# Moving the gated delta rule's elementwise work from GpSimd to VectorE: all of it in layer 0, three operations in layer 1

## The chip, the cores and the metric

The kernel runs on one core of a Trainium2 chip. A core has a matrix engine (TensorE, PE in the profile), a vector engine (VectorE, DVE), an engine for activations and copies (ScalarE, ACT), a general engine (GpSimd, POOL) and a queue that starts the loads of weights (SyncE, SP). Each engine works through its own instructions strictly in the order in which they were put down; semaphores make one engine wait for another. The metric is the time of one execution on the device in microseconds: the median of three executions of the kernel before is 1779.97 us (1774.64 to 1780.54).

## What is computed

Two layers of a diffusion backbone over 256 context tokens and 256 latent tokens, 1024 channels, all in float32. In each layer a modulated RMS norm is projected at once to the inputs of three mixers (latent attention, windowed attention, and a bidirectional gated delta rule); their outputs are gated, merged and projected, and a gated MLP with a depthwise convolution follows. The change is in the delta rule alone. It works on chunks of 64 tokens, 8 heads of 64 channels, forwards and backwards:

```python
gam = jnp.cumsum(g, axis=-1)
decay = jnp.exp(jnp.minimum(gam[..., :, None] - gam[..., None, :], 0.0))
a_mat = jnp.where(strict, jnp.einsum('nbhid,nbhjd->nbhij', kb, k) * decay, 0.0)   # kb = k * beta
t_mat = a_mat + jnp.eye(C)
wy = triangular_solve(t_mat, rhs, left_side=True, lower=True, unit_diagonal=True)
qk = jnp.where(incl, jnp.einsum('nbhid,nbhjd->nbhij', q, k) * decay, 0.0)
def step(S, xs):                                   # over the 4 chunks
    v_new = u_c - w_c @ S
    o = (q_c * exp(gam_c)) @ S + qk_c @ v_new
    S = S * exp(g_last) + (k_c * exp(g_last - gam_c)).T @ v_new
y = rmsnorm(o, o_norm) * silu(z)
```

## The kernel before, in words

**Projections.** Weights come by DMA into `raw` tiles (three buffers, mostly 128x1024). ScalarE rounds each to `wh` (L189), VectorE makes the remainder `wl = raw - wh` (L179, four buffers), and TensorE forms each product from three matmuls (L199 to L201: `wh` times the high part of the activations, `wh` times the low part, `wl` times the high part). L201 can't start on a tile before VectorE has made its `wl`. Accumulators are in PSUM, 3 buffers named `mm` and 5 named `g`.

**Delta rule.** Streams `s` are the context (0) and the latent tokens (1). `gdn_decay(s)` runs over two halves `tl` and two phases `ph`: `rg` (L803) spreads the log decays, a matmul (L808) sums them, L809 takes the difference `d` out of PSUM, L813 to L816 make the masked decays `Eq` for q·k, L819 to L821 those for k·k, L824 makes `bm` (mask times beta), `times_k` multiplies 64x64 products of keys into a tile (matmuls L839; the multiplication is on the line of a helper, L131), and L828 forms `N = d*bm`. `gdn_solve(s)` inverts the unit triangular matrices: VectorE transposes `N` in 32x32 blocks, runs a chain of 60 dependent multiply and add operations on `gtmp` and `W`, transposes back, TensorE joins the blocks (matmuls L877 and L905), and L915 scales the result `XT` by beta. `gdn_scan(s)` takes 4 steps: the state product (matmul L935, L938 and L940 on VectorE), `pvn` (matmul L951), `vp` (L955), the decay of the state (L958), its update (matmul L965, addition L970), and the output (matmuls L980, L985 and L986). `gdn_out` scales the output rows (L1009) ahead of the transposes L1014. A layer needs `qk` for the context only if it isn't the last.

**The order of the work.** These parts are generators that yield a number of microseconds; `chain` puts that much projection work (the "filler", with its loads and splits) between two parts, so TensorE has matmuls while VectorE computes the decays. Each engine's final order comes from a scheduler that goes by the tiles' dependencies and by priorities: `times_k` and the transposes and chain of `gdn_solve` are recorded through a helper with a raised priority, so that the profile puts them on the helper's line, L131. Where a group of the profile has line L131 with tiles `s<-s,g` of 128x512 it is `times_k`'s multiplication; with `gtmp` it is the solve's chain. The delta rule of layer 0 stands between about 86 and 405 us of the profile, that of layer 1 between about 1175 and 1405 us.

## Time and profile before

| what | value |
|---|---|
| median of three executions | 1779.97 us (1774.64 to 1780.54) |
| the profiled execution | 1780.76 us, its span 1779.0 us |
| TensorE | 1679.0 us busy, mean granted clock 0.968 |
| VectorE | 1133.4 us busy |
| ScalarE | 769.2 us busy |
| GpSimd | 300.4 us busy, 281 instructions |

TensorE is busy nearly throughout, so the places that count are those where it waits, or where it runs at a lower granted clock. An engine's mean load over the span says little about a stretch; the windows show each engine's busy time stretch by stretch, the waits show for whom TensorE stood still, and the rows in time show what VectorE did meanwhile.

### The profile page before, as it was taken

The numbers are of one execution on the slowest core, as the hardware profiler recorded it, in microseconds if no ns is written. First come the engines' busy times: TensorE is split into PE (matmuls) and PEld (weight loads), VectorE is DVE, ScalarE is ACT, GpSimd is POOL, SyncE is SP. The second block draws the span as 40 slices with busy tenths as digits, with TensorE's granted clock in tenths as the row PEclk, the third lists the DMA queues.
The fourth block names the chain that finished last, engine by engine and source line by source line (L and its number), as shares of the span: only waits on it lengthen the run. The fifth ranks groups of instructions, "written<-read, shape, count | busy, mean of one in ns | idle before, by whom it ended". The sixth has DMA issues, their size and how long they took to land. (4 is left out here: it accounts for less than half of the span.)

```text
span 1779.0 us, 31557 instructions
## 1 busy us (share of the span) xinstructions
PE 1679.0 (94%) x12723; PEld 1363.7 (77%) x12723; DVE 1133.4 (64%) x2159; ACT 769.2 (43%) x1371; POOL 300.4 (17%) x281
## 2 busy tenths in 40 slices
PE   7989988999999999999999999999898899999997
PEld 4768765776556888768888888778787667999997
DVE  3897595474865643545535553699796776677684
ACT  3644312233755333324313432464523475555463
POOL 1040411221200222001100112030502310213010
PEclk8999998998999999999999999999998999999999
DMA  9423326333043633663333343434352223745663
GB/s 346 115 72 107 96 73 190 72 75 111 25 143 122 210 119 120 253 231 96 98 95 103 95 141 120 125 92 141 90 120 58 60 77 98 236 144 182 185 185 124
DMA packets 216944, 228.75 MB, mean 129 GB/s; under 512 B 51228, under 2 KB 195422, under 8 KB 215646
## 3 DMA queue, kind: packets, MB, share of 16 engines
q1 hardware_dynamic: 211582, 220.11, 40.5%
q10 hardware_dynamic: 4928, 6.56, 1.0%
q8 instruction: 100, 1.64, 0.4%
q14 instruction: 46, 0.38, 0.1%
q0 software_dynamic: 288, 0.06, 0.0%
HBM read 213.85 MB, written 11.80 MB: 127 GB/s over the span
## 5 line engine op out<-in xcount | busy, mean ns | idle before, releaser
L179 DVE TENSOR_TENSOR wl<-raw,wh 128x1024 fp32r<-128x1024 f32 (+2 forms) x294 | 364.3, 1239 | 250.2 <-ACT wh L189 248.6
L189 ACT CAST wh<-raw 128x1024 fp32r<-128x1024 f32 (+2 forms) x294 | 298.4, 1017 | 422.3 <-PE mm L200 220.5
L199 PE MATMUL mm<-xnh,wh 128*128 128x512 f32 (+2 forms) x1072 | 380.3, 356 | 5.8 <-ACT wh L189 2.4
L201 PE MATMUL mm<-xnh,wl 128*128 128x512 f32 (+2 forms) x1072 | 375.9, 353 | 1.3 <-DVE wl L179 1.3
L200 PE MATMUL mm<-xnl,wh 128*128 128x512 f32 (+2 forms) x1072 | 376.0, 351 | 0.1
L199 PEld LDWEIGHTS mm<-xnh,wh 128*128 128x128 f32 (+1 forms) x1072 | 206.3, 193 | 39.4 <-issue 7.0
L201 PEld LDWEIGHTS mm<-xnh,wl 128*128 128x128 f32 (+1 forms) x1072 | 205.9, 192 | 31.5 <-issue 3.3
L200 PEld LDWEIGHTS mm<-xnl,wh 128*128 128x128 f32 (+1 forms) x1072 | 206.1, 192 | 27.8 <-issue 2.9
L199 PE MATMUL g<-xnh,wh 128*128 128x256 f32 (+1 forms) x496 | 167.3, 340 | 1.4 <-ACT xnh L405 1.4
L200 PE MATMUL g<-xnl,wh 128*128 128x256 f32 (+1 forms) x496 | 166.4, 337 | 0.2 <-DVE xnl L406 0.2
L201 PE MATMUL g<-xnh,wl 128*128 128x256 f32 (+1 forms) x496 | 166.1, 336 | 0.0
L201 PE MATMUL mm<-s,wl 128*128 128x256 f32 (+1 forms) x458 | 150.0, 328 | 0.6 <-DVE wl L179 0.6
L199 PE MATMUL mm<-s,wh 128*128 128x256 f32 (+1 forms) x458 | 150.1, 329 | 0.4 <-DVE s L534 0.3
L200 PE MATMUL mm<-s,wh 128*128 128x256 f32 (+1 forms) x458 | 149.6, 327 | 0.1
L1616 POOL TENSOR_TENSOR b<-b,b 128x512 f32<-128x512 f32 (+1 forms) x44 | 54.3, 1234 | 442.5 <-DVE b L1600 381.6
L199 PEld LDWEIGHTS g<-xnh,wh 128*128 128x128 f32 x496 | 94.6, 192 | 15.0 <-issue 3.3
L199 PE MATMUL g<-s,wh 128*128 128x512 f32 (+1 forms) x304 | 102.8, 338 | 0.0
L201 PEld LDWEIGHTS g<-xnh,wl 128*128 128x128 f32 x496 | 94.6, 191 | 10.5 <-issue 1.2
L200 PEld LDWEIGHTS g<-xnl,wh 128*128 128x128 f32 x496 | 94.7, 191 | 10.1 <-DVE xnl L406 0.8
L200 PE MATMUL g<-s,wh 128*128 128x512 f32 (+1 forms) x304 | 102.2, 336 | 0.0
L201 PE MATMUL g<-s,wl 128*128 128x512 f32 (+1 forms) x304 | 102.2, 336 | 0.0
L199 PEld LDWEIGHTS mm<-s,wh 128*128 128x128 f32 x458 | 87.2, 191 | 8.8 <-DVE s L534 1.1
(285 smaller groups left out, 2743.6 us busy)
## 6 DMA issues: line engine op xcount, KB each, us to landing
raw<-in_w_in_dram SPq DMA_DIRECT2D x92, 512.0 KB
raw<-in_ffn_up_dram SPq DMA_DIRECT2D x80, 512.0 KB
s<-in_w_mod_dram SPq DMA_DIRECT2D x64, 512.0 KB
raw<-in_w_mod_dram SPq DMA_DIRECT2D x32, 512.0 KB
raw<-in_ffn_down_dram SPq DMA_DIRECT2D x32, 512.0 KB
raw<-in_w_out_dram SPq DMA_DIRECT2D x16, 512.0 KB
raw<-in_ffn_down_dram SPq DMA_DIRECT2D x16, 384.0 KB
spill<-s SPq DMA_DIRECT2D x4, 1024.0 KB
```

The source lines that it names most:

```text
L179: self.nc.vector.tensor_tensor(out=out, in0=x, in1=h.bitcast(F32), op=ALU.subtract)
L189: nc.scalar.copy(H, raw)
L199: mm(ps, lhsT=wH, rhs=xH, start=start, stop=False)
L200: mm(ps, lhsT=wH, rhs=xL, start=False, stop=False)
L201: mm(ps, lhsT=wL, rhs=xH, start=False, stop=stop)
L1616: nc.gpsimd.tensor_tensor(out=y[:, cs], in0=y[:, cs], in1=av[t][:, cs], op=ALU.mult)
```

## The change

A method `side()` returns VectorE in layer 0 and GpSimd in layer 1 (`narrow` is set at the start of a layer and is true in the last). The operations L803, L816, L824, L958 and L985 go through it, so they change engine in layer 0 alone. L828, L915 and L1009 are written for VectorE in both layers. The memory clears of the solve (L892) stay on GpSimd, as do the operations of attention and of the norms. In numbers, 50 instructions change engine in layer 0 (8 each of L803, L816, L824 and L915, 6 of L958, 4 each of L828, L985 and L1009) and 14 in layer 1 (4 of L828, 8 of L915, 2 of L1009). From the new method on, a line of the changed kernel has a number larger by 4: L828 is L832 there.

```diff
--- before.py
+++ after.py
@@ -792,6 +792,10 @@
         self.gt = dict(g=g, be=be, si=si, so=so, sk=sk, gam=gam, eg=eg, ekl=ekl, egl=ev)
         yield 2.0
 
+    def side(self):
+
+        return self.nc.gpsimd if self.narrow else self.nc.vector
+
     def gdn_decay(self, s, has_q):
 
         nc, gt = self.nc, self.gt
@@ -800,7 +804,7 @@
         for tl in range(2):
             rg = self.b4([128, 2, 8, 64])
             for ph in range(2):
-                nc.gpsimd.tensor_tensor(out=rg[:, ph], in0=gt["g"][:, s, ph, tl, :].unsqueeze(2).to_broadcast([128, 8, 64]),
+                self.side().tensor_tensor(out=rg[:, ph], in0=gt["g"][:, s, ph, tl, :].unsqueeze(2).to_broadcast([128, 8, 64]),
                                         in1=self.con(f"triJ{ph}").unsqueeze(1).to_broadcast([128, 8, 64]), op=ALU.mult)
             d = self.b4([128, 2, 8, 64])
             for ph in range(2):
@@ -813,7 +817,7 @@
                 self.pri(nc.vector, "hpd").tensor_scalar(out=Eq, in0=d, scalar1=0.0, scalar2=None, op0=ALU.max)
                 self.pri(nc.scalar, "hpd").activation(out=Eq, in_=Eq, func=AF.Exp, scale=-1.0)
                 for ph in range(2):
-                    nc.gpsimd.tensor_tensor(out=qk[:, tl, ph], in0=Eq[:, ph],
+                    self.side().tensor_tensor(out=qk[:, tl, ph], in0=Eq[:, ph],
                                             in1=self.con(f"mincl{ph}").unsqueeze(1).to_broadcast([128, 8, 64]), op=ALU.mult)
             for ph in range(2):
                 self.pri(nc.vector, "hpd").tensor_scalar(out=d[:, ph], in0=d[:, ph], scalar1=self.con("sgn")[:, ph:ph + 1], scalar2=0.0,
@@ -821,11 +825,11 @@
             self.pri(nc.scalar, "hpd").activation(out=d, in_=d, func=AF.Exp)
             bm = self.b4([128, 2, 8, 64])
             for ph in range(2):
-                nc.gpsimd.tensor_tensor(out=bm[:, ph], in0=gt["be"][:, s, ph, tl, :].unsqueeze(2).to_broadcast([128, 8, 64]),
+                self.side().tensor_tensor(out=bm[:, ph], in0=gt["be"][:, s, ph, tl, :].unsqueeze(2).to_broadcast([128, 8, 64]),
                                         in1=self.con("nms").unsqueeze(1).to_broadcast([128, 8, 64]), op=ALU.mult)
             yield self.P["dec1"]
             self.times_k(s, tl, 0, d)
-            nc.gpsimd.tensor_tensor(out=N[:, tl], in0=d, in1=bm, op=ALU.mult)
+            nc.vector.tensor_tensor(out=N[:, tl], in0=d, in1=bm, op=ALU.mult)
             yield self.P["dec2"]
 
     def times_k(self, s, tl, which, t):
@@ -912,7 +916,7 @@
                 self.evac(q, Xv[qs, tl, ph, :, 1 - q % 2, :], pq[qs, tl])
         for ph, tl in STEPS:
             hs = slice(ph * 64, ph * 64 + 64)
-            nc.gpsimd.tensor_tensor(out=XT[hs, tl, ph], in0=XT[hs, tl, ph],
+            nc.vector.tensor_tensor(out=XT[hs, tl, ph], in0=XT[hs, tl, ph],
                                     in1=gt["be"][hs, s, ph, tl, :].unsqueeze(2).to_broadcast([64, 8, 64]), op=ALU.mult)
         yield self.P["sol4"]
 
@@ -955,7 +959,7 @@
                 self.pri(nc.vector, "hps").tensor_tensor(out=vp, in0=pvn, in1=bc("sk"), op=ALU.mult)
                 Sn = self.b2([128, 2, 4, 64])
                 if St is not None:
-                    nc.gpsimd.tensor_tensor(out=Sn, in0=St, in1=gt["egl"][:, s, ph, tl].unsqueeze(3).to_broadcast([128, 2, 4, 64]), op=ALU.mult)
+                    self.side().tensor_tensor(out=Sn, in0=St, in1=gt["egl"][:, s, ph, tl].unsqueeze(3).to_broadcast([128, 2, 4, 64]), op=ALU.mult)
                 for hf in range(2):
                     hs = slice(hf * 64, hf * 64 + 64)
                     psu = self.ps([128, 4, 64], "g")
@@ -982,7 +986,7 @@
                     t = self.b2([128, 8, 64])
                     state_product(1, t)
                     if n >= 2:
-                        nc.gpsimd.tensor_tensor(out=t, in0=t, in1=o3, op=ALU.add)
+                        self.side().tensor_tensor(out=t, in0=t, in1=o3, op=ALU.add)
                     self.pri(nc.vector, "hps").tensor_tensor(out=o3, in0=t, in1=pqk, op=ALU.add)
                 else:
                     self.pri(nc.vector, "hps").tensor_copy(o3, pqk)
@@ -1006,7 +1010,7 @@
         self.rstd(r, ss, 1.0 / 64, [128, 2, 8])
         nc.vector.tensor_tensor(out=r, in0=r, in1=qr, op=ALU.mult)
         for tl in range(2):
-            nc.gpsimd.tensor_tensor(out=hd(oacc[:, tl, :]), in0=hd(oacc[:, tl, :]), in1=r[:, tl, :].unsqueeze(2).to_broadcast([128, 8, 64]), op=ALU.mult)
+            nc.vector.tensor_tensor(out=hd(oacc[:, tl, :]), in0=hd(oacc[:, tl, :]), in1=r[:, tl, :].unsqueeze(2).to_broadcast([128, 8, 64]), op=ALU.mult)
         yield Lat(self.P["w_o"])
         for tl in range(2):
             pf = self.ps([128, 4, 128], "g")
@@ -1294,7 +1298,7 @@
         nc, i = self.nc, self.ins
         if l:
             self.P = dict(P, **P["l1"])
-        last = l == DEPTH - 1
+        last = self.narrow = l == DEPTH - 1
         lat, full = slice(S, T), slice(0, T)
         oc = lat if last else full
         n = self.qw = S if last else T
```

The scheduler's order changes with it. On VectorE, in the first decay of layer 0, before: the second pair of `times_k`'s multiplications, the transposes of `N` (`s_141`), and two splits of weights (`wl_1125`, `wl_1161`); `s_171` is the solve's `W`.

```order
L131 TENSOR_TENSOR s_159_875<-s_159_875,g_911 128x8x64
L131 TENSOR_TENSOR s_159_875<-s_159_875,g_921 128x8x64
L131 STREAM_TRANSPOSE s_171_966<-s_141_768 128x1024
L665 SCALAR_TENSOR_TENSOR b_170_958<-mm_847,vec_86,b_170_958 128x2x255
L131 STREAM_TRANSPOSE s_171_966<-s_141_768 32x1024
L667 SCALAR_TENSOR_TENSOR b_170_958<-mm_847,vec_86,b_170_958 128x2x255
L131 STREAM_TRANSPOSE s_171_966<-s_141_768 32x1024
L179 TENSOR_TENSOR wl_1125<-raw_1122,wh_1124 128x1024
L131 TENSOR_TENSOR gtmp_970<-s_171_966 128x30
L699 TENSOR_REDUCE sm_1019<-b_181_1020 128x8
L131 TENSOR_TENSOR s_171_966<-s_171_966,gtmp_970 128x30
L699 TENSOR_REDUCE sm_1019<-b_182_1023 128x8
```

And the same place in the changed kernel:

```order
L179 TENSOR_TENSOR wl_1125<-raw_1122,wh_1124 128x1024
L820 TENSOR_TENSOR s_142_769<-s_162_882,cst 128x512 x2
L131 TENSOR_TENSOR s_159_875<-s_159_875,g_911 128x8x64
L131 TENSOR_TENSOR s_159_875<-s_159_875,g_921 128x8x64
L699 TENSOR_REDUCE sm_1019<-b_181_1020 128x8
L832 TENSOR_TENSOR s_141_768<-s_159_875,s_163_890 128x1024
L699 TENSOR_REDUCE sm_1019<-b_182_1023 128x8
L131 STREAM_TRANSPOSE s_171_966<-s_141_768 128x1024
L346 TENSOR_SCALAR sm_1028<-sm_1019 128x16
L131 STREAM_TRANSPOSE s_171_966<-s_141_768 32x1024 x2
L347 TENSOR_SCALAR sm_1029<-sm_1028 128x16
L179 TENSOR_TENSOR wl_1161<-raw_1158,wh_1160 128x1024
```

The first of the two splits, formerly behind the transposes, is now ahead of them, the second is still behind them, and `N` (L832) and the masked decays (L820) are in VectorE's own row; L699 has moved ahead of the transposes.

On VectorE, in the second decay of layer 0 and at the start of the scan, before: `s_297` is `d`, `s_142` and `s_282` are the `qk` of the two streams, `s_281` is `N`, and L955 is the scan's `vp`.

```order
L131 TENSOR_TENSOR s_297_1927<-s_297_1927,g_1973 128x8x64
L131 STREAM_TRANSPOSE s_325_2121<-s_281_1854 128x1024
L131 TENSOR_TENSOR s_142_769<-s_142_769,g_2008 128x8x64
L131 TENSOR_TENSOR s_142_769<-s_142_769,g_2018 128x8x64
L131 TENSOR_TENSOR s_142_769<-s_142_769,g_2028 128x8x64
L131 TENSOR_TENSOR s_142_769<-s_142_769,g_2038 128x8x64
L131 TENSOR_TENSOR s_282_1855<-s_282_1855,g_2048 128x8x64
L131 TENSOR_TENSOR s_282_1855<-s_282_1855,g_2058 128x8x64
L131 TENSOR_TENSOR s_282_1855<-s_282_1855,g_2068 128x8x64
L131 TENSOR_TENSOR s_282_1855<-s_282_1855,g_2078 128x8x64
L131 STREAM_TRANSPOSE s_325_2121<-s_281_1854 32x1024 x2
L955 TENSOR_TENSOR b_327_2150<-g_2089,gtb_754 128x512
```

The changed kernel:

```order
L131 TENSOR_TENSOR s_282_1855<-s_282_1855,g_2068 128x8x64
L131 TENSOR_TENSOR s_282_1855<-s_282_1855,g_2078 128x8x64
L131 TENSOR_TENSOR s_297_1927<-s_297_1927,g_1963 128x8x64
L131 TENSOR_TENSOR s_297_1927<-s_297_1927,g_1973 128x8x64
L959 TENSOR_TENSOR b_327_2150<-g_2089,gtb_754 128x512
L832 TENSOR_TENSOR s_281_1854<-s_297_1927,s_301_1942 128x1024
L179 TENSOR_TENSOR wl_2236<-raw_2233,wh_2235 128x1024
L131 STREAM_TRANSPOSE s_325_2121<-s_281_1854 128x1024
L972 COPY b_328_2152<-g_2153 128x256
L131 STREAM_TRANSPOSE s_325_2121<-s_281_1854 32x1024 x2
L972 COPY b_328_2152<-g_2163 128x256
```

`times_k`'s eight multiplications for `qk` now come first, then the pair for `N`, then the scan's `vp` (L959), and the transposes stand behind it and behind a split.

On VectorE, in the second decay of layer 1: `s_1898` is `d`, `s_1879` is `N`, `s_1880` is `qk`.

```order
L131 TENSOR_TENSOR s_1898_11316<-s_1898_11316,g_11372 128x8x64
L131 TENSOR_TENSOR s_1898_11316<-s_1898_11316,g_11382 128x8x64
L179 TENSOR_TENSOR wl_11521<-raw_11518,wh_11520 128x1024
L131 STREAM_TRANSPOSE s_1923_11505<-s_1879_11225 128x1024
L131 TENSOR_TENSOR s_1880_11226<-s_1880_11226,g_11448 128x8x64
L131 TENSOR_TENSOR s_1880_11226<-s_1880_11226,g_11458 128x8x64
L131 TENSOR_TENSOR s_1880_11226<-s_1880_11226,g_11468 128x8x64
L131 TENSOR_TENSOR s_1880_11226<-s_1880_11226,g_11478 128x8x64
L131 STREAM_TRANSPOSE s_1923_11505<-s_1879_11225 32x1024 x2
L955 TENSOR_TENSOR b_1930_11536<-g_11488,gtb_10178 128x512
```

The changed kernel:

```order
L131 TENSOR_TENSOR s_1898_11316<-s_1898_11316,g_11372 128x8x64
L131 TENSOR_TENSOR s_1898_11316<-s_1898_11316,g_11382 128x8x64
L179 TENSOR_TENSOR wl_11521<-raw_11518,wh_11520 128x1024
L832 TENSOR_TENSOR s_1879_11225<-s_1898_11316,s_1902_11331 128x1024
L131 TENSOR_TENSOR s_1880_11226<-s_1880_11226,g_11448 128x8x64
L131 TENSOR_TENSOR s_1880_11226<-s_1880_11226,g_11458 128x8x64
L131 TENSOR_TENSOR s_1880_11226<-s_1880_11226,g_11468 128x8x64
L131 TENSOR_TENSOR s_1880_11226<-s_1880_11226,g_11478 128x8x64
L131 STREAM_TRANSPOSE s_1923_11505<-s_1879_11225 128x1024
L959 TENSOR_TENSOR b_1930_11536<-g_11488,gtb_10178 128x512
L131 STREAM_TRANSPOSE s_1923_11505<-s_1879_11225 32x1024 x2
```

The multiplications for `qk` now come before the first transpose, and `vp` (L959) before the other two.

## Rows read from the trace of the kernel before

**Rows 1.** The page, part 1: busy time of each engine, share, instructions.

```profile
PE 1679.0 (94%) x12723; PEld 1363.7 (77%) x12723; DVE 1133.4 (64%) x2159; ACT 769.2 (43%) x1371; POOL 300.4 (17%) x281
```

**Rows 2.** Windows: microseconds, busy PE, PEld, DVE, ACT, POOL, PEclk, DMA, GB/s.

```profile
86.00:122.00 36.00, 30.28 (x176) 22.79 (x177) 32.10 (x55) 20.37 (x42) 21.27 (x18) 0.91 0.22 64
...
100.00:150.00 50.00, 46.45 (x209) 38.15 (x208) 45.56 (x108) 26.69 (x50) 9.82 (x9) 0.96 0.30 85
1200.00:1250.00 50.00, 48.03 (x384) 41.79 (x383) 47.88 (x107) 25.29 (x49) 1.04 (x2) 1.00 0.44 127
```

**Rows 3.** TensorE's waits, 86 to 122 us: total, times, longest.

```profile
PE g L688 <- ACT s L671: 3.5, 1, 3.5
PE g L839 <- DVE s L809: 2.1, 1, 2.1
```

**Rows 4.** VectorE's groups: line, tiles, shapes, count, busy us, mean ns, idle before.

```profile
L179 DVE TENSOR_TENSOR wl<-raw,wh 128x1024 fp32r<-128x1024 f32 x264 | 338.9, 1284 | 244.4 <-ACT wh L189 243.0
...
L131 DVE TENSOR_TENSOR s<-s,g 128x512 f32<-128x512 f32 x28 | 17.5, 676 | 5.4 <-ACT s L821 5.4
...
L1282 DVE TENSOR_TENSOR s<-s,s 64x512 fp32r<-64x512 f32 x8 | 5.5, 686 | 0.2
```

**Rows 5.** GpSimd's groups, the same columns.

```profile
L828 POOL TENSOR_TENSOR s<-s,s 128x1024 f32<-128x1024 f32 x8 | 20.3, 2535 | 9.3 <-DVE s L131 4.8 <-ACT b L698 2.4 <-ACT wh L189 1.4
L803 POOL TENSOR_TENSOR s<-gtb,cst 128x512 f32<-128x512 f32 x16 | 18.8, 1194 | 127.1 <-DVE gtb L753 126.9
```

**Rows 6.** VectorE in time, 85 to 118 us: start, duration, line [idle, releaser].

```profile
85.55 0.19 DVE L756 TENSOR_SCALAR gtb<-gtb 128x64 f32<-128x64 f32 x1
...
87.09 1.09 DVE L764 TENSOR_SCALAR gtb<-gtb,cst 128x32 f32<-128x32 f32 x1
...
98.64 2.49 DVE L819 TENSOR_SCALAR s<-s,cst 128x512 f32<-128x512 f32 x1
...
101.71 0.61 DVE L819 TENSOR_SCALAR s<-s,cst 128x512 f32<-128x512 f32 x1
...
107.34 2.03 DVE L131 STREAM_TRANSPOSE s<-s 128x1024 f32<-128x1024 f32 x1 [2.61 <-POOL s L828]
...
117.50 1.22 DVE L179 TENSOR_TENSOR wl<-raw,wh 128x1024 fp32r<-128x1024 f32 x1
```

**Rows 7.** TensorE's waits, 195 to 260 us.

```profile
PE g L839 <- DVE s L131: 4.3, 1, 4.3
PE g L951 <- DVE b L940: 2.2, 1, 2.2
```

**Rows 8.** VectorE in time, 222 to 236 us.

```profile
224.25 1.90 DVE L131 STREAM_TRANSPOSE s<-s 128x1024 f32<-128x1024 f32 x1 [2.55 <-POOL s L828]
```

**Rows 9.** TensorE's waits, 260 to 293 us.

```profile
PE mm L593 <- DMA raw<-in_w_mod_dram: 5.8, 8, 1.3
```

**Rows 10.** TensorE's waits, 380 to 405 us.

```profile
PE g L1014 <- POOL s L1009: 2.6, 4, 1.3
```

**Rows 11.** TensorE's waits, 1175 to 1215 us.

```profile
PE mm L201 <- DVE wl L179: 1.0, 1, 1.0
```

**Rows 12.** VectorE in time, 1190 to 1197 us.

```profile
1192.44 3.15 DVE L179 TENSOR_TENSOR wl<-raw,wh 128x1024 fp32r<-128x1024 f32 x1
```

**Rows 13.** TensorE's waits, 1270 to 1300 us.

```profile
PE g L965 <- DVE b L955: 7.4, 1, 7.4
```

**Rows 14.** VectorE in time, 1274 to 1290 us.

```profile
1276.61 1.22 DVE L179 TENSOR_TENSOR wl<-raw,wh 128x1024 fp32r<-128x1024 f32 x1
1280.13 2.00 DVE L131 STREAM_TRANSPOSE s<-s 128x1024 f32<-128x1024 f32 x1 [2.30 <-POOL s L828]
...
1288.33 0.69 DVE L955 TENSOR_TENSOR b<-g,gtb 128x512 f32<-128x512 f32 x1
```

**Rows 15.** TensorE's waits, 1330 to 1360 us.

```profile
PE g L877 <- DVE s L131: 3.5, 1, 3.5
PE g L951 <- POOL s L915: 1.6, 1, 1.6
```

## The prediction

> **What bounds the kernel now.** I read the engines' busy time first, then the windows, then for each stretch of the delta rule what TensorE waited for, and last the rows in time of VectorE there. TensorE is busy for 1679.0 of 1779.0 us, VectorE for 1133.4, GpSimd for 300.4 [rows 1]. So the change can save only where TensorE stands still, and GpSimd's own load matters nowhere by its size. The windows show that VectorE's mean of 64% hides full stretches: 45.6 of 50 us from 100 to 150 us, 32.1 of 36 in the first decay, 47.9 of 50 at 1200 us [rows 2]. There the engine that is to receive the work has nearly no room. The order shows the rest: VectorE makes the weight remainders `wl` in the same row as the delta rule, and whatever is put into that row delays them.
>
> The question is therefore a balance in each stretch: a GpSimd operation is slow and its consumer waits for it, but its time is not VectorE's.
>
> **The price of the moved work.** On VectorE a two-input operation of 128x512 takes 0.68 us (mean of 28, `times_k`'s multiplication), of 64x512 0.69, and of 128x1024 1.22 where nothing disturbs it, 1.28 in the mean [rows 4, 6]. On GpSimd L803 takes 1.19 and L828 2.54 [rows 5]. The trace does not show these very operations on VectorE: the multiplication read one operand from PSUM, the moved ones read both from SBUF, so 0.68 and 1.22 are my values by the same shape, with the longer GpSimd times as the upper end and half of these values as a lower end, for a shape that might run faster. By these ends a decay's sum below, 10.6 us, would be 19.4 or 5.3; I stay with 10.6, since all rows of VectorE on such shapes agree to 0.01 us. In layer 0 the change moves 46 operations of 512 elements and 4 of 1024: 46 x 0.68 + 4 x 1.22 = 36.2 us. In layer 1 it is 10 of 512 and 4 of 1024: 6.8 + 4.9 = 11.7 us. VectorE thus gains 48 us of work, to about 1181 before any refund.
>
> **The refund.** Some of VectorE's operations run long while GpSimd works. L819 takes 2.49 us at 98.64 and 0.61 at 101.71; L764 takes 1.09 on 32 elements a row, L756 0.19 on 64 [rows 6]. Four such small operations stand there (L762 and L764, twice each): at 0.9 us each 3.6 us come back if GpSimd is the cause, and 1.9 of the one long L819. A third part is VectorE's own idle time for L828, 2.6 us before the first transpose [rows 6]. Together that is 8.1 us in the first decay.
>
> The Trainium skill has a rule for the first two parts (GPSIMD Engine Reference, 1. Specifications: the SBUF interfaces are shared with VectorE, with contention for VectorE instructions in a two-port mode or with two SBUF inputs). The long L819, a one-input operation, agrees with it [rows 6]; with the rule the refund would be 8.1 us, without it only the idle 2.6.
>
> **Part by part, on TensorE's path.**
>
> First decay of layer 0 (86 to 122 us). VectorE receives 4 each of L803, L816 and L824 and 2 of L828: 12 x 0.68 + 2 x 1.22 = 10.6 us; less the refund of 8.1 it ends 2.5 us later. TensorE waits 2.1 us for L809 [rows 3], and the granted clock is 0.91 in this stretch [rows 2]. That wait largely goes, as `rg` is made in 0.68 us instead of 1.19 and L809 is no longer behind four slowed small operations. Queued behind the new work are the splits: the one that began at 117.50 [rows 6] still stands behind the transposes, and the solve's chain with it. The solve itself has room, as `chain` puts projection work between its parts. But the split is what L201 waits for, and 2.5 us of lateness comes there as a wait of which TensorE's earlier arrival makes a little more. The 3.5 us wait for L671 [rows 3] is ScalarE's and moves, not vanishes. I take -1.5 us; bounds -5.6 (both waits gone) and +8.5 (all 10.6 lands on TensorE, less 2.1).
>
> Second decay and start of the scan of layer 0 (195 to 260). The same 10.6 us come in; out go the 2.55 us of idle for L828 [rows 8] and the slowed operations. TensorE's 4.3 us wait for `times_k` and 2.2 us for L940 [rows 7] stand here. The first nearly goes, because the eight multiplications for `qk` now precede `N` and the transposes. The scan's first steps then come to a VectorE that is only about 2 us earlier (2.55 of idle and 1.9 of one slowed operation come back, less two `N` of 1.22), so the second wait grows to about 4.3: 6.5 before, 4.3 after, -2.2 us. Bounds -6.5 and +6.3 (10.6 less 4.3). Behind it TensorE is paced by the loads of `w_mod` from 260 to 293 us, 5.8 us of waits [rows 9]; the loads are asked for by SyncE in unchanged order as buffers come free, so the stretch moves as a whole. The 10 operations L958 and L985 (10 x 0.68 = 6.8 us) fall there and shortly behind it, where those waits and VectorE's slack cover them: 0; without the cover +6.8. L915 in layer 0 has the same kind of cover, 0.
>
> `gdn_out`: TensorE waits 2.6 us for L1009 in layer 0 [rows 10]. Two operations of 0.68 instead of 1.19 each and less of a gap leave about 0.6: -2.0 (0 to -2.6). Layer 1 has one pair of these operations instead of two: counted at a quarter, -0.5.
>
> Layer 1, first decay (1175 to 1215): only L828 moves, 2 x 1.22 us. TensorE waits 1.0 us for a split there [rows 11]; that split takes 3.15 us at 1192.44 [rows 12] instead of 1.22, beside GpSimd's L828, which goes. It gains 1.9 and gets one L828 of 1.22 ahead of it: -0.7 (-1.0 to +2.4).
>
> Layer 1, second decay. The long wait is 7.4 us, for `vp` on L955 [rows 13]. VectorE's row there: a split at 1276.61, idle 2.30 us for L828, transpose, `times_k`, two transposes, and `vp` only at 1288.33 [rows 14]. Afterwards it is split 1.22, N 1.22, four multiplications 2.7, transpose 2.0, `vp`: 1276.61 + 7.1 = 1283.7, 4.6 us earlier, of which another L828 ahead (1.22) may take a part. So this wait shrinks to 3 or 4. But the two transposes behind `vp` and the whole solve still hang on VectorE. Their sum of work is the same plus 1.22 for N, less the idle 2.30, so the solve starts only about 1 us sooner, and its end is what L877 waits for, 3.5 us before [rows 15]. What TensorE gains at `vp` it therefore stands at L877, apart from that 1 us and a shorter `wl` or two. I take -1.5 (-7.4 to +2.4, the two L828 wholly on the path).
>
> L915 behind that solve: 1.6 us of TensorE's wait for it [rows 15], but VectorE is copying results at that time. -0.5 (0 to -1.6).
>
> Sum: -1.5 - 2.2 - 2.0 - 0.5 - 0.7 - 1.5 - 0.5 = -8.9 us. The profiled execution took 1780.76 us, its span and 1.8 around it; 1780.8 - 8.9 = 1771.9, so 1772. The median of the runs before, 1779.97, is 0.8 below the profiled one, which is less than these terms are known to.
>
> **The rivals.**
>
> *All the waits go.* If the refund is larger than counted, each wait behind a moved operation ends: 2.1 + 4.3 + 2.2 + 2.6 + 0.5 + 1.0 + 7.4 + 1.6 = 21.7 us, so 1759. For it: the 0.91 clock of the first decay would rise as well. Against: the solve of layer 1 hangs on VectorE's sum of work, which does not fall.
>
> *The waits only move.* In every term above the work that VectorE gains is as long as what it no longer waits for; the first decay and the solve of layer 1 return all that the others save, and only `gdn_out` is left, -2.5: 1778, not to be told from no change (5.3 us, 0.3%, is about what a measurement of this kernel can tell). For it: 47.9 of 50 us [rows 2].
>
> *VectorE becomes the bound in layer 0: slower.* If its slow operations are not GpSimd's doing, or if the idle gaps were absorbed anyway, only the idle time comes back. The two decays of layer 0 then put 10.6 us each in front of the splits: +8.5 in the first and +3.7 in the second (10.6 less 4.3 and less 2.6), the other terms stay at -5.2: +7.0, 1788. The point from which it decides is the split after the transposes in the first decay: later than about 122 us it holds TensorE up by more than the waits removed.
>
> By itself stands a sentence of the Trainium skill (Perfetto Trace Analysis, Optimizing Scalar/DVE Operations): with VectorE saturated, offloading "even" to GpSimd may make sense, though the two share a read port and it "might not help". Its first half speaks against this change, and its time would be this rival's 1788.
>
> *Nothing to see because little is moved* I leave out: 64 instructions change engine, in both layers.
>
> **How the numbers follow.** The forecast (-4 to -14 us) has a chance of 0.45, all waits gone 0.12, waits only moved 0.24, slower 0.19. The likeliest one's own range is 1766 to 1777. From the cases: faster by over 0.3% (below 1774.6) 0.41 of the first and all of the second, 0.53; within 0.3% 0.04 and 0.24, 0.28; slower 0.19. The range of 8 in 10 goes from 1758, where all waits are gone, to 1787, just under the slower case's 1788; about half of that case and the ends of the first two, some 0.15 to 0.2, are left out.
>
> **What would show it.** VectorE's L819, L762 and L764 of the first decay at 0.6 and 0.2 us would show the refund; if they stay long, the slower case gains. TensorE's wait at `times_k` of the second decay should be below 1 us, that at the scan's first `pvn` about 4. In layer 1 the wait for `vp` should be 3 to 4 us and that at the solve's matmuls 6 or more; if the latter stays at 3.5 the gain is about 5 us larger. The waits for L1009 should be below 1 us in sum. The forecast is wrong if TensorE waits for a split by 5 us or more in the first decay of layer 0, or if VectorE's busy time there is 36 of 36 with TensorE's below 30.

## The result, and the profile after

The changed kernel took 1760.03 us (median of 4 executions, 1758.41 to 1762.26) against 1779.98: a ratio of 0.989, 95% interval 0.9869 to 0.9911. Three more comparisons with fresh runs gave 0.9924 (0.9905 to 0.9944), 0.9918 (0.9893 to 0.9942) and 0.9926 (0.9905 to 0.9947); all 22 executions have a median of 1762.5 us. All four intervals hold a ratio of about 0.991, some 16 us. The forecast was -8: right in sign, and the time within its range, but half of the size or less.

The page's first part, to be set against [rows 1]:

```profile
PE 1668.4 (95%) x12723; PEld 1355.3 (77%) x12723; DVE 1160.7 (66%) x2223; ACT 777.4 (44%) x1377; POOL 217.0 (12%) x217
```

TensorE ran the same 12723 matmuls. The span is 20.7 us shorter: 10.6 us less busy time and 10.1 us less idle time (100.0 before, 89.9 after). The matmuls are the same, and the mean granted clock is 0.976 instead of 0.968. This split runs through all that follows.

Where it came from is read from stretches between the same two matmuls of TensorE. First the kernel before, then the changed one (columns as in [rows 2]): second decay and scan start of layer 0, the stretch paced by `w_mod`, the rest of the scan, output of the delta rule, and then the 692 us up to layer 1's delta rule, in which nothing changed.

```profile
195.60:255.80 60.20, 53.59 (x539) 42.27 (x540) 48.25 (x84) 17.85 (x22) 24.58 (x19) 0.94 0.20 62
255.80:292.40 36.60, 28.11 (x536) 17.88 (x534) 24.46 (x61) 5.07 (x11) 3.31 (x3) 0.94 0.72 227
292.40:350.50 58.10, 55.92 (x801) 42.92 (x801) 27.38 (x45) 14.62 (x21) 12.82 (x12) 0.89 0.32 81
350.50:430.00 79.50, 74.58 (x559) 57.27 (x563) 47.34 (x104) 26.76 (x44) 14.48 (x15) 0.98 0.30 73
430.00:1121.80 691.80, 680.72 (x3528) 526.88 (x3529) 362.53 (x650) 280.96 (x501) 89.70 (x79) 0.99 0.41 134
```

```profile
192.60:247.60 55.00, 52.74 (x536) 40.64 (x536) 49.25 (x87) 21.84 (x25) 1.04 (x2) 1.00 0.22 68
247.60:282.40 34.80, 29.16 (x539) 18.91 (x537) 30.84 (x79) 5.07 (x11) 0.00 (x0) 0.90 0.68 223
282.40:336.10 53.70, 52.21 (x807) 40.41 (x803) 30.33 (x52) 14.65 (x21) 4.28 (x4) 0.97 0.38 96
336.10:413.00 76.90, 72.34 (x556) 56.14 (x555) 51.24 (x111) 26.77 (x44) 7.28 (x9) 1.00 0.32 77
413.00:1104.00 691.00, 680.55 (x3529) 526.56 (x3530) 362.26 (x650) 281.27 (x501) 89.49 (x79) 0.99 0.41 134
```

The first four are shorter by 5.2, 1.8, 4.4 and 2.6 us, the last by 0.8. In the third, TensorE's idle time fell from 2.2 to 1.5 us only; its granted clock rose from 0.89 to 0.97. These are two single executions. The third stretch took about 57 us in the trace of a kernel whose layer 0 is as before (layer 1 alone, below) and about 56 in another trace of the changed kernel, so the 4.4 us are not a steady gain. The last stretch is the noise to have in mind. The same stretch of the changed kernel in another comparison:

```profile
411.90:1108.40 696.50, 685.24 (x3529) 529.10 (x3530) 362.33 (x650) 281.20 (x501) 89.38 (x79) 0.98 0.41 133
```

It is 5.5 us longer, with the same instructions and 0.98 instead of 0.99 as mean clock.

**First decay of layer 0.** VectorE in time (start, duration, line, [idle before, releaser]) and TensorE's wait, against [rows 3, 6]:

```profile
85.53 0.30 DVE L764 TENSOR_SCALAR gtb<-gtb,cst 128x32 f32<-128x32 f32 x1
...
103.38 0.88 DVE L823 TENSOR_SCALAR s<-s,cst 128x512 f32<-128x512 f32 x2
...
109.47 1.29 DVE L131 TENSOR_TENSOR s<-s,g 128x512 f32<-128x512 f32 x2 [2.28 <-ACT s L825]
...
113.00 2.05 DVE L131 STREAM_TRANSPOSE s<-s 128x1024 f32<-128x1024 f32 x1
...
119.18 1.22 DVE L179 TENSOR_TENSOR wl<-raw,wh 128x1024 fp32r<-128x1024 f32 x1
```

```profile
PE mm L201 <- DVE wl L179: 4.5, 2, 3.5
```

L764 takes 0.30 us instead of 1.09, two L823 together 0.88 (formerly L819, 2.49 for one), and there is no idle time ahead of the transpose. But VectorE now waits 2.28 us ahead of `times_k`'s multiplication, for ScalarE's exponential (L825, formerly L821): its idle time in this decay is 3.5 us, and was 3.3. TensorE's waits for L809 and for ScalarE's L671 are gone; new is the one for the split at 119.18, behind the transposes.

**Second decay.** What VectorE did before, which the rows ahead of the prediction don't show, and then the same operations after:

```profile
204.14 1.89 DVE L179 TENSOR_TENSOR wl<-raw,wh 128x1024 fp32r<-128x1024 f32 x1 [3.42 <-ACT wh L189]
...
212.76 2.13 DVE L813 TENSOR_SCALAR s<-s 128x1024 f32<-128x1024 f32 x1
214.81 2.06 DVE L179 TENSOR_TENSOR wl<-raw,wh 128x1024 fp32r<-128x1024 f32 x1
216.79 2.50 DVE L819 TENSOR_SCALAR s<-s,cst 128x512 f32<-128x512 f32 x2
...
253.73 0.42 DVE L938 TENSOR_TENSOR b<-g,gtb 128x256 f32<-128x256 f32 x1
```

```profile
201.08 1.23 DVE L179 TENSOR_TENSOR wl<-raw,wh 128x1024 fp32r<-128x1024 f32 x1 [1.99 <-ACT wh L189]
...
212.20 1.22 DVE L179 TENSOR_TENSOR wl<-raw,wh 128x1024 fp32r<-128x1024 f32 x1
213.34 0.69 DVE L817 TENSOR_SCALAR s<-s 128x1024 f32<-128x1024 f32 x1
...
214.54 0.88 DVE L823 TENSOR_SCALAR s<-s,cst 128x512 f32<-128x512 f32 x2
...
224.96 0.69 DVE L959 TENSOR_TENSOR b<-g,gtb 128x512 f32<-128x512 f32 x1
...
246.15 0.75 DVE L942 TENSOR_TENSOR b<-g,gtb 128x256 f32<-128x256 f32 x2
```

```profile
PE g L955 <- DVE b L944: 1.4, 1, 1.4
...
PE g L843 <- DVE s L131: 0.2, 1, 0.2
```

Before, a split took 1.89 and 2.06 us, L813 2.13, a pair of L819 2.50; after, 1.23, 1.22, 0.69 and 0.88. `vp` (L959) starts at 224.96 instead of 234.98, and the transposes, 5.9 us that stood ahead of it, stand behind it. From the start of the stretch to the state product of the scan's second step (L938, now L942) VectorE needs 53.6 us instead of 58.1. VectorE's idle time in the stretch, by the windows above, is 5.8 us instead of 12.0. TensorE's waits of 4.3 and 2.2 us [rows 7] are 0.2 and 1.4.

**Behind it.** The waits for `w_mod` [rows 9], then those ahead of the output's transposes [rows 10]:

```profile
PE mm L593 <- DMA raw<-in_w_mod_dram: 3.2, 4, 1.2
```

```profile
PE g L1018 <- DVE sm L1009: 1.1, 1, 1.1
PE g L1018 <- DVE s L1013: 0.4, 1, 0.4
```

The scaling itself is L1013 now; L1009 is a small operation ahead of it, which was on VectorE before too. Together the waits are 1.5 us instead of 2.6.

**Layer 1, second decay.** TensorE's waits up to 1280 us and from there to 1337 us, against [rows 13, 15], and VectorE's `N` and `vp`, against [rows 14]:

```profile
PE g L969 <- DVE b L959: 1.9, 1, 1.9
PE g L939 <- DVE b L972: 1.6, 1, 1.6
```

```profile
PE g L881 <- DVE s L131: 4.0, 1, 4.0
PE g L955 <- DVE s L534: 2.2, 1, 2.2
PE g L955 <- DVE s L919: 1.3, 1, 1.3
```

```profile
1258.26 1.22 DVE L832 TENSOR_TENSOR s<-s,s 128x1024 f32<-128x1024 f32 x1
...
1263.65 0.65 DVE L959 TENSOR_TENSOR b<-g,gtb 128x512 f32<-128x512 f32 x1
```

`vp` follows `N` in 5.4 us, and TensorE's wait for it fell from 7.4 to 1.9; a new one of 1.6 stands behind VectorE's copy of the state (L972). The end of the solve keeps it for 4.0 instead of 3.5, and two new waits of 2.2 and 1.3 stand behind VectorE's copies (L534) and its own scaling of `XT` (L919, formerly GpSimd's, 1.6 [rows 15]).

### The profile page after: what moved, and what is told of

It reads as the page before. It is cut to its first block, busy times and chain, and to the rows that moved or that the text cites. A ratio compares the mean times of both kernels' runs of the same rounds, so it can differ in the third digit from the quotient of the medians.

```text
span 1758.3 us, 31525 instructions
## 1 busy us (share of the span) xinstructions
PE 1668.4 (95%) x12723; PEld 1355.3 (77%) x12723; DVE 1160.7 (66%) x2223; ACT 777.4 (44%) x1377; POOL 217.0 (12%) x217
## 5 line engine op out<-in xcount | busy, mean ns | idle before, releaser
L179 DVE TENSOR_TENSOR wl<-raw,wh 128x1024 fp32r<-128x1024 f32 (+2 forms) x294 | 357.7, 1217 | 236.9 <-ACT wh L189 235.7
L200 PEld LDWEIGHTS g<-xnl,wh 128*128 128x128 f32 x496 | 94.7, 191 | 10.1 <-DVE xnl L406 0.8
```

Of the source, the lines that this page charges most:

```text
L179: self.nc.vector.tensor_tensor(out=out, in0=x, in1=h.bitcast(F32), op=ALU.subtract)
L200: mm(ps, lhsT=wH, rhs=xL, start=False, stop=False)
```

## The experiments

Most kernels are the changed one with the choice of engine written out for each operation and layer:

```diff
-    def side(self):
-        return self.nc.gpsimd if self.narrow else self.nc.vector
+    def side(self, k):
+        on = (('rg','qk','bm','N','Sn','t','XT','out'), ('N','XT','out'))[self.narrow]
+        return self.nc.vector if k in on else self.nc.gpsimd
```

`rg`, `qk`, `bm` and `N` are the decays' operations, `Sn` and `t` the scan's, `XT` and `out` L915 and L1009. The two lists are those of layer 0 and layer 1. "Theory clock" in the expectations: a removed wait gives back its own length and the half-clock time that TensorE ran behind it. "Theory scan": the missing gain is the latency of L958 and L985.

**Layer 0 alone**, `on = ((all eight), ())`:

> The 50 moves of layer 0 alone; layer 1 as before. Theory 'clock': the terms that I priced by waits alone get a second part, since TensorE ran at the half clock for about 34 us of layer 0's delta rule before and 14 us after; layer 0 then carries -16 to -18 us: about 1763. Theory 'scan' (the missing gain is the latency of L958 and L985, which I priced at nothing): the same total, 1763, but it must then be seen in the run with the scan alone. The prediction's own terms would give -5.7 here: 1774.

Measured: 1765.91 us against 1779.15, ratio 0.9934 (0.9911 to 0.9956). **Layer 1 alone**, `on = ((), ('N','XT','out'))`:

> The 14 moves of layer 1 alone. All theories: -3 us, 1777 (the prediction's terms sum to -3.2); TensorE's wait for vp falls from 7.4 to about 2 and the next waits, at the solve's matmuls and behind, take most of it back. If layer 1 alone gains 8 or more, the gain of layer 0 is the smaller part and both theories fall.

Measured: 1773.74, ratio 0.9972 (0.9954 to 0.999). The two together make 0.9906, as the changed kernel has it; layer 0 carries two thirds, and neither is as small as its terms in the forecast (-5.7 and -3.2), though layer 1's interval holds its term.

**The decays of layer 0 alone**, `on = (('rg','qk','bm','N'), ())`:

> Only L803, L816, L824 and L828 of layer 0 go to VectorE. Prediction's terms: -3.7, 1776. Theory 'clock': the waits of the two decays (4.3 + 2.2 + part of 2.1) and the half clock behind them: -7 to -10, 1770 to 1773. Theory 'scan': -4, 1776, the rest being in the scan's run.

Measured: 1775.28, ratio 0.9982 (0.9963 to 1.0002), not clear of no change. **The scan of layer 0 alone**, `on = (('Sn','t'), ())`:

> Only L958 and L985 of layer 0 go to VectorE (10 operations). Prediction: 0, 1780. Theory 'scan': VectorE waited 7 us in all for L985 and TensorE behind it, so -6 to -9, 1771 to 1774, with fewer half-clock microseconds between 290 and 350 us. Theory 'clock': -1 to -3, 1777 to 1779, as no long wait of TensorE stands at these operations.

Measured: 1779.0, ratio 1.0008 (0.9993 to 1.0024): theory "scan" falls. The traces show which wait belongs to which part. TensorE's waits from 191 to 262 us, with the decays moved and then with the scan moved:

```profile
PE g L843 <- DVE s L131: 0.2, 1, 0.2
```

```profile
PE g L843 <- DVE s L131: 4.3, 1, 4.3
```

The wait for `times_k` goes with the decays and stays with the scan. The stretch of 60.2 us there is 55.0 to 55.5 us in all nine traces of kernels that have both decays of layer 0 wholly on VectorE and nothing added (this one and the four of the changed kernel included), and 59.4 to 60.3 in the three other traces of kernels that have not. Why the whole run of the decays alone is only 3.9 us faster is not settled: in its trace the stretch that took 54.7 us between 1252 and 1307 us before, with the same instructions, took 57.3, but that is one execution.

**L915 and L1009 of layer 0 alone**, `on = (('XT','out'), ())`:

> Only L915 and L1009 of layer 0 go to VectorE. Layer 0 as a whole gained 0.66%, its decays 0.18%, its scan 0. If parts add up, these 12 operations carry the rest, -0.4 to -0.5%, 1771; their waits of TensorE (2.6 us at the transposes) and the clock behind them are all that the trace before offers, so the theory 'clock' by itself expects -0.2 to -0.3%, 1774 to 1776, and then the rest comes only from several parts together.

Measured: 1776.39 against 1778.79, ratio 0.9993 (0.998 to 1.0005), not clear of no change either. Beside it ran the changed kernel again:

> The changed kernel once more, on the chip of the next three, to know its size beside a spread of 1771 to 1786 us in the kernel before. Both theories: 0.987 to 0.991 of the time before. If it is 0.99 to 0.993, the sum of the two layers' runs (-0.66% and -0.28%) explains it without an interplay.

Measured: 1766.94, 0.9924, so at the upper end of what was expected. **Decays, L915 and L1009 together**, `on = (('rg','qk','bm','N','XT','out'), ())`:

> Layer 0 without the scan: the decays, L915 and L1009 on VectorE, layer 1 as before. The parts measured -0.18% (decays) and -0.07% (L915 and L1009), the whole of layer 0 -0.66%. If the parts add up: 0.997 to 0.998, 1773 to 1775. If they are worth more together, as TensorE's clock is not lost in the second place once it is not lost in the first: 0.993 to 0.995, 1766 to 1770.

Measured: 1771.84 against 1776.79, ratio 0.9967 (0.9951 to 0.9983). The parts, -0.18% and -0.07%, make -0.25%; together -0.33%: they add up within their intervals, and no interplay is needed for these two. **The changed kernel with the scan of layer 0 left on GpSimd**, `on = (('rg','qk','bm','N','XT','out'), ('N','XT','out'))`:

> The changed kernel, but L958 and L985 of layer 0 stay on GpSimd. The scan alone moved nothing, so both theories that count waits expect the changed kernel's time, 1760 to 1763. If the scan's move is worth something only once the rest of layer 0 is on VectorE, this is slower by 4 us or more; if its 10 operations burden a fuller VectorE, it is faster.

Measured: 1765.1, ratio 0.9933 (0.9915 to 0.9951), beside 0.9924 for the changed kernel on the same chip: no difference. So the 10 operations of the scan can stay on either engine; a gain of 0.2% from them, once the rest has moved, is not excluded by the intervals.

**GpSimd's load put back without its latency.** The changed kernel, in which GpSimd repeats 24 of the moved operations into tiles that are dead by then:

```diff
                         in1=gr, op=ALU.subtract)
+                if not self.narrow:
+                    nc.gpsimd.tensor_tensor(out=rg[:, ph], in0=gt["g"]..., in1=self.con(f"triJ{ph}")..., op=ALU.mult)
```

and the same behind the uses of `Eq` and of `bm`.

> The changed kernel, with GpSimd repeating L807, L820 and L828 of layer 0 (24 operations) into tiles that are dead by then; nothing waits for the results but the later users of those buffers. This puts GpSimd's load beside VectorE back without its latency. If VectorE's long operations before came from GpSimd's work, single-input operations and splits beside these 24 run long again (L823 at 1 to 2.5 us instead of 0.47) and the run is 2 to 8 us slower than the changed kernel; if not, it is within 2 us.

Measured: 1771.73, ratio 0.997 (0.9954 to 0.9987), 4.8 us slower than the changed kernel beside it (0.9924). TensorE's wait in the first decay, and VectorE in the second (here L838 is `N`, L179 a split, L820 the former L813):

```profile
PE mm L201 <- DVE wl L179: 6.8, 1, 6.8
...
216.34 2.11 DVE L838 TENSOR_TENSOR s<-s,s 128x1024 f32<-128x1024 f32 x1
...
219.57 2.09 DVE L179 TENSOR_TENSOR wl<-raw,wh 128x1024 fp32r<-128x1024 f32 x1
221.58 1.54 DVE L820 TENSOR_SCALAR s<-s 128x1024 f32<-128x1024 f32 x1
```

`N` takes 2.11 us instead of 1.22, the split 2.09, L820 1.54 instead of 0.69, while nobody waits for a result of GpSimd. The stretch of the second decay is 58.6 us instead of 55.0, and the wait for the split in the first decay is 6.8 instead of 3.5. Splits and the former L813 thus run long again when GpSimd works beside them. L829 (the former L819) kept its 0.44 us, so for L819 this run does not show the cause; the single-input operation that ran long here is L820. In the first decay the stretch is 101.9 us instead of 97.7.

**A wait filled.** The kernel before, with matmuls of constants into the unused half of product tiles that exist already, which keep TensorE busy where it waits:

```diff
+    def busy(self, p, n):
+        for _ in range(n):
+            self.nc.tensor.matmul(p[:, 4:8], lhsT=self.con("bones"), rhs=self.con("cswa"), start=True, stop=True)
...
+            if not self.narrow and s == 1 and which == 1 and tl == 0 and pr == 0:
+                self.busy(pf, 14)
```

> The kernel before, with matmuls of constants put into two of TensorE's long waits: 14 behind the fifth product tile of the second decay of layer 0 (its wait there is 4.3 us, and the granted clock is at half for 6.8 us from about 223 us) and 24 ahead of the scan's first update in layer 1 (wait 7.4 us, half for 10.2 us from about 1285 us). They write the unused half of tiles that exist already; every wait and every operation of the other engines stays. Theory 'clock' (a wait costs itself and then a stretch at the half clock): the two stretches lose their half-clock time, half of 6.8 and of 10.2, so -6 to -8.5 in these stretches and about 1772 in all. If only waits count: no change, or 1 us slower for matmuls that outlast the wait.

Measured: 1792.57, ratio 1.0079 (1.0056 to 1.0102). This trial was badly sized: each of these matmuls took 0.45 us, so 14 took 6.3 us in a wait of 4.3, and the 24 in layer 1 began only behind another wait and took 12.3 us. The mended one has 9, and none in layer 1:

> The kernel before with 9 matmuls of constants (0.45 us each at the full clock as measured, 4.05 us) in the one wait of 4.3 us in the second decay of layer 0. The earlier trial had 14 there, 6.3 us. Theory 'clock': the wait stays as long, the 6.8 us at half behind it stay away, and the way from the first product of the five tiles to the first scan product is 1 to 2 us shorter than 8.99 us; of this VectorE, which is behind, may take a part back at the scan's first update, so -1 to -3 in the stretch from 196 to 256 us and hardly more than -0.2% in all. If only waits count: 9 us on that way and no change.

Measured: 1782.67 against 1776.79, ratio 1.003 (1.0014 to 1.0046). TensorE in time without the filler matmuls, first the kernel before, then the one with the filled wait (L833 are the added matmuls, L844 `times_k`, L975 the scan's update):

```profile
219.84 2.60 PE L839 MATMUL g<-s 64*64 64x64 f32 x80
226.77 2.10 PE L839 MATMUL g<-s 64*64 64x64 f32 x44 [4.33 <-DVE s L131]
...
236.15 0.98 PE L965 MATMUL g<-b,s 64*64 64x64 f32 x32
```

```profile
218.17 2.64 PE L844 MATMUL g<-s 64*64 64x64 f32 x80
220.74 4.15 PE L833 MATMUL g<-cst 128*128 128x256 f32 x18
225.20 1.88 PE L844 MATMUL g<-s 64*64 64x64 f32 x48 [0.31 <-DVE s L131]
...
235.36 0.97 PE L975 MATMUL g<-b,s 64*64 64x64 f32 x32 [1.55 <-DVE b L962]
```

Its next wait, in the second step of the scan, stood at 2.2 us before [rows 7]:

```profile
PE g L958 <- DVE b L947: 5.7, 1, 5.7
```

The half clock behind the filled wait is gone (the mean granted clock from 195 to 256 us is 0.99 where the stretch from 195.6 to 255.8 us had 0.94, and the 48 matmuls of `times_k` take 1.88 us instead of 2.10 for 44). But from the first `times_k` to the scan's update it is 17.2 us instead of 16.3: TensorE comes sooner and then waits 1.6 us for `vp`, which in this kernel also stands behind a split and four multiplications. The larger loss comes after it: in VectorE's new order 48 operations of the solve's chain stand ahead of the second step's state product instead of 38, and TensorE waits 5.7 us for it instead of 2.2. The trial therefore does not show what the clock alone is worth, since VectorE's order shifted with it.

**The wait for the split.** The changed kernel, with the mask of the context's q·k decays left on GpSimd:

```diff
-                    self.side('qk').tensor_tensor(out=qk[:, tl, ph], in0=Eq[:, ph],
+                    (nc.gpsimd if s == 0 else self.side('qk')).tensor_tensor(out=qk[:, tl, ph], in0=Eq[:, ph],
```

> The changed kernel, but the mask of the context's q.k decays (L820, 4 operations in the first decay of layer 0), which nobody needs before the second decay, stays on GpSimd. VectorE then reaches the weight split ahead of the transposes, for which TensorE waited 3.5 us in the changed kernel. Theory 'VectorE's row' (the wait is its fullness): the wait of 3.5 goes and the half clock behind it, -4 to -6 beside the changed kernel. Rival: four GpSimd operations slow VectorE's neighbours by as much as they free: 0.

Measured: 1762.35 against 1761.6 for the changed kernel beside it, ratios 0.9902 (0.9876 to 0.9929) and 0.9918. Those runs of the changed kernel had this on record:

> The changed kernel again, to stand beside the next two on the same chip: 0.989 to 0.992 of the time before by both earlier readings.

TensorE's wait in the first decay and the stretch from its start, and below that the stretch of the changed kernel:

```profile
PE mm L201 <- DVE wl L179: 1.1, 1, 1.1
...
32.00:123.30 91.30, 88.90 (x486) 66.43 (x485) 75.22 (x175) 52.31 (x103) 5.74 (x6) 1.00 0.41 125
```

```profile
31.50:129.20 97.70, 91.59 (x486) 67.09 (x485) 78.52 (x180) 56.34 (x107) 1.04 (x2) 0.98 0.39 118
```

The wait of 3.5 us is 1.1 and the stretch 6.4 us shorter, at a clock of 1.00 instead of 0.98. Again, with the changed kernel beside it:

> The changed kernel with the context's mask of q.k decays in layer 0 left on GpSimd, again. In the profile its first stretch was 7 us shorter than in the changed kernel (idle 2.4 instead of 5.8 us, no half clock), but the medians were the same (1762.35 and 1761.6). If the 7 us are real, -4 to -7 beside the changed kernel; if they were that execution's luck with the clock, 0.

> The changed kernel beside the next two: 0.989 to 0.992 of the time before.

Measured: 1761.91 (0.9917, 0.9892 to 0.9941) and 1764.3 (0.9926). The stretch is 91.3 us in both profiles, but over 12 executions the median is 1761.9 against 1762.5 for 22 of the changed kernel: the expected -4 to -7 did not show in the time, and that it is faster is not shown; a likely reason stands below, with the clock.

**The rest of layer 1 on VectorE too**, `on = ((all eight), (all eight))`:

> The changed kernel with L807, L820, L828, L962 and L989 of layer 1 on VectorE too. VectorE was busy 47.9 of 50 us there before. My slower rival (VectorE becomes the bound) expects it here: 3 to 8 us slower than the changed kernel, with longer waits for splits around 1180 us and for the solve at 1316. If contention is the larger price, it is 2 to 5 us faster.

Measured: 1779.41 against 1777.85, ratio 1.0007 (0.9988 to 1.0026), 18 us slower than the changed kernel beside it. TensorE's waits from 1300 to 1345 us:

```profile
PE g L881 <- DVE s L131: 6.9, 1, 6.9
PE g L955 <- DVE b L944: 5.2, 2, 4.9
```

The solve's end keeps it for 6.9 us instead of 4.0, and a state product for 4.9. The slower rival is real, one layer further on: 28 more operations on a VectorE that is nearly full take back all that 64 had gained, more than the 3 to 8 us expected. Which of the 28 do it was not tested.

## Why the prediction was half right

**Sign and price held, the refund in part.** The moved operations take 0.68 and 1.22 us on VectorE, as taken. In the first decay L762 and L764 gave back 2.8 us and the four L819 3.1, but not the idle time: what went ahead of the transpose, 2.6 us, came back ahead of `times_k`, where VectorE now waits 2.3 us for ScalarE. That is 5.9 us instead of 8.1, and the split behind the transposes comes 35.3 us after the operations ahead of the decay (L749) instead of 32.1, so 3.2 later where 2.5 was forecast. The wait for it was named, and the stretch is 1.8 us shorter in the first trace (99.5 to 97.7; 1.5 forecast). The output's stretch gave 2.6 us (2.0 forecast), but TensorE's idle time fell there by 0.4 only; the rest is the clock, 0.98 to 1.00. Layer 1's second decay went by its steps: TensorE's idle time fell by 4.3 us around `vp` and rose by 2.3 from the solve's end on, in three waits (4.0, 2.2, 1.3) and not at L877 alone. That makes -2.0, as the terms -1.5 and -0.5 had it.

**The step that failed: the second decay and what lies behind it in layer 0**, -2.2 and 0 in the forecast, -5.2 and -6.2 in the first trace (the `w_mod` stretch and the rest of the scan). Two things in it were wrong.

First, VectorE's way to the second wait. The forecast had VectorE 2.0 us sooner there (2.55 of idle time and 1.9 of one slowed operation, less two `N`); it was 4.6 sooner, and each part was off. Counted without the overlap of neighbours, 10.9 us of moved work stand ahead of the state product, L915 among it, and not 2.4. The slowed operations, two splits, L813 and the L819, give back 4.8 and not 1.9: I had read VectorE's rows of the first decay for them, and not those from 204 to 222 us. The idle time fell by 6.2 and not by 2.55. And 11 operations of the solve's chain, 4.5 us, went behind the state product (38 ahead of it before, 27 after): 10.9 - 4.8 - 6.2 - 4.5 = -4.6. So the second wait did not grow from 2.2 to 4.3 but fell to 1.4. Two runs bear on these parts. The decays alone, whose trace has that stretch at 55.5 us, show that the decays carry it; GpSimd's repeats, which bring 3.6 us of it back, show what its presence beside VectorE is worth there. No run parts the idle time from the order.

Second, the granted clock, a term that the forecast put at nothing. It priced waits alone, so it was a forecast of idle time. As a sum it came close: -8.9 forecast, -10.1 measured (100.0 to 89.9; in the other three traces of the changed kernel 88 to 93). That is in part luck, for the terms are off both ways: -2.2 against -4.3 in the second decay, 0 against -2.9 at `w_mod`, -2.0 against -0.4 at the output. I had [rows 2] with a clock of 0.91 in the first decay in hand and left it to a rival. From 292 to 350 us a mean clock of 0.89 over 58.1 us is 12.8 us at the half level (2 x 0.11 x 58.1), which cost half of that, and TensorE's idle time was 2.2: a term of 0 there looked safe.

What the clock made of the whole can be estimated, as every execution has its span and its mean granted clock on record. Their product is about what the execution would have taken at the full clock (a wait at the half level counts half in it), the rest is what the lower level cost. The means are 1719.8 and 56.6 us over 85 executions of the kernel before, 1713.9 and 48.1 over the 22 of the changed one. So of 14.4 us between the mean spans some 6 are waits and some 8 the clock, with standard errors of 0.7 and 1.4. GpSimd's repeats have 1719.6 and 51.7: they give back all of the 6. The traces agree for layer 0's delta rule: in the three of kernels whose layer 0 decays and solve are as before, 26 to 30 us of idle time and 34 to 37 us at half; in the four of the changed kernel 21 to 24 and 10 to 20.

**The rivals.** "All the waits go", 1759, is nearest to the first measurement and not what happened: TensorE's idle time fell by 10 us, not by 21.7, and the rest is clock. "VectorE becomes the bound" was wrong about layer 0 and right about layer 1 with more work. The sentence of the Trainium skill behind it (Perfetto Trace Analysis, Optimizing Scalar/DVE Operations) is borne out there alone; in the first decay of layer 0 VectorE was nearly as full (32.1 of 36 us against 47.9 of 50), and the stretch did not get longer by the moved work. The other rule of the Trainium skill that the prediction used (GPSIMD Engine Reference, 1. Specifications: the SBUF interfaces are shared, with contention for VectorE instructions in a two-port mode or with two SBUF inputs) agrees with the rows: single-input operations went from 1.09 to 0.30 us, two-input ones from 2.06 to 1.22, and L809, which has only one operand in SBUF and the other in PSUM, took 0.68 us before and 0.69 after. Whether the single-input ones ran in a two-port mode no run here shows.

**What stays open.** Why the lower clock cost 8 us less: the trial that was to isolate it changed VectorE's order. And whether the mask left on GpSimd is worth having: its 12 executions have 1708.9 us at the full clock, 5 less than the changed kernel, and lost 50.9 to the clock, 2.8 more (standard errors 1.2 and 2.4), so that the shorter first stretch is likely real and in part taken back by the clock.

## What to carry to other kernels

Before work is moved off a slow engine, add up what that engine's presence costs its neighbour, over every stretch where both run and not only the first: here some 6 us in one decay and 5 in the other, about half of the 10.6 us that the moved work costs in each. Then follow the receiving engine's new order to the operation that the bounding engine waits for: here 4.5 us of other work moved behind it. A sum of waits forecasts idle time, not time. Where the matrix engine runs at a lower granted clock behind its waits, give the clock a term of its own, and a range as wide as unchanged stretches differ between executions. And stop where the receiving engine is paced by a long chain of its own: the same move helped in layer 0 and lost everything in layer 1.

## What the runs showed of the hardware

A VectorE operation beside GpSimd's can run several times as long: L764 on 32 elements a row took 1.09 us beside one and 0.30 without, and a single-input operation on 128x1024 (L813) 2.13 and 0.69. The difference, 0.8 and 1.4 us, is of the length of one GpSimd operation of 128x512, 1.19 us in the mean [rows 5], and not in proportion to VectorE's own work. Repeating 24 such GpSimd operations beside an otherwise equal kernel cost it 4.8 us. A stretch of 692 us with unchanged instructions took 691 to 697 us in the traces of the kernel before and of the changed one, with 10 to 11 us of idle time and a mean granted clock of 0.98 to 0.99, which is more than several of the terms argued about here. A matmul of 128x128 by 128x256 in float32 is two instructions in the trace and took 0.45 us at the full clock.
